# One hybrid attention block on one core: feed-forward modulation by row sums, reordered opening loads, earlier gate spills, and a root kept together at the norm

## Chip, core and metric

The kernel runs on one core of a Trainium2 chip (trn2). The metric is the device time of one execution in microseconds (us), as the median of three runs. The before kernel takes 1754.09 us (1749.22 to 1755.53). Everything is float32 with 256 tokens and a model width of 2048.

## Reference

```python
c_act = silu(c)
mod = (c_act @ ada_w + ada_b)            # 6 vectors of 2048
shift_m, scale_m, gate_m, shift_f, scale_f, gate_f = mod
h = rmsnorm(x, norm_mix_g) * (1 + scale_m) + shift_m
p = h @ w_in                             # gla q,k,v,g,gk | mla cq,ckv,kr | two gates
y_gla = (rmsnorm(gla(q,k,v,decay)) * silu(g)) @ gla_wo
y_mla = causal_mla(cq, ckv, kr) @ mla_wo
x = x + gate_m * ((sigmoid(ga)*y_gla + sigmoid(gb)*y_mla) @ w_out)
h = rmsnorm(x, norm_ffn_g) * (1 + scale_f) + shift_f
g, u = split(h @ ffn_w_in)
x = x + gate_f * ((silu(g)*u) @ ffn_w_down)
return rmsnorm(x, final_norm_g)
```

## The kernel before, in words

**Weights.** Every weight tile is loaded as 128 partitions of 1024 float32 (512 KB, `load_raw`, L102, issued by SP into a rotating list of `raw` tiles) and split in two parts: ACT casts it to a high part (L111) and DVE subtracts to a low part (L114). PE then multiplies high by high, low by high and high by low (`form_a`, L179 to L181; `form_b`, L190 to L192). One tile, called a half below, feeds 12 matmuls of 512 columns. There are three buffers for the high and the low parts.

**Stages.** (1) The opening (L429 to L474) loads x, its squares and root, transposes x with PE (`x_blocks`, L360), and works out shift and scale of the mixer. (2) The input projection runs in four rounds over the 2048 input rows, so that it can start when few rows of h exist; `jobs` is the list of 16 output blocks, `orders` the order of a round. In round 3 (the last) jobs 11 to 15 are five gate blocks, which lie in slots 4 and 6. (3) The attention: eight `mla_pair`s, with four GLA heads (`gla_att`) woven in by lanes that `tick()` advances. Pair 0 writes its projections into slot 6 (L647). (4) The GLA output gate with `gla_out` per head, then `mla_wo`, `gla_wo` and `w_out`, four blocks of eight halves each. (5) The norm, the feed-forward, and the last norm.

**Modulation.** There are two ways to a vector of `mod`. `ada_dots` (L258 to L279) loads rows of a transposed copy `ada_t`, one 512 KB tile being half of 128 rows, and makes their sums with a DVE instruction that multiplies with the broadcast `crow` and accumulates (L269): two tiles give 128 values, one per partition. It serves the mixer's shift and scale (m = 0, 1). `ada_steps` (L288 to L334) loads `ada_w` as it is, multiplies and adds on DVE (L304, two per tile), sums over partitions on POOL (`partition_all_reduce`, L314), and for m = 3 and 4 brings the result into columns with four more DVE instructions (L321). It serves m = 2 to 5. `pace` sets how many such steps a `tick()` (one per half) issues from the list `bg`; a step issues one tile.

**POOL** also does the rope angles in the opening (`rope_angles`, L364 to L400) and the root of each GLA head (`rsqrt_mean` with `G`, L213 to L216). The store of the summed gate goes out on SP (L317), the five gate spills on POOL after round 3 (L579).

**Order.** Each engine runs its instructions in one order, which a scheduler sets at build time; `keep_in_program_order` (`pin`) and `follow` bind single instructions.

Of the kernel before, what the change touches and what calls it, by code (L numbers as in the profile page):

```python
# [51 lines left out]
def tile_block(ctx: ExitStack, tc: tile.TileContext, x, positions, ada_w, ada_t, ada_b, w_in, gla_gk_w, gla_wo,  # L52
# [33 lines left out]

    def raw_tile():
# [17 lines left out]
    def split_raw(raw, kk, cols, perm=None):  # L105
# [115 lines left out]

    def rows_of(col, dst, pinned=False):
# [3 lines left out]
        for t in range(2):  # L226
            pin(V.tensor_scalar(out=d[:, t * P:(t + 1) * P], in0=ident, scalar1=col[:, t:t + 1], scalar2=None,
                                op0=ALU.mult))
# [26 lines left out]
    nc.gpsimd.dma_start(out=scr[:, 324:357], in_=cf[:, 256:289])  # L255
# [4 lines left out]
    def ada_dots(k, now=False):  # L260
        for m in (1, 0):
            c = m * 16 + k
            part = sb(1, "md", 4)
            for hf in range(2):
                raw = raw_tile()
                d = nc.sync.dma_start(out=raw, in_=ada_t[m * D + k * P:m * D + (k + 1) * P, hf * 1024:(hf + 1) * 1024])

                def dot(raw=raw, hf=hf, c=c, part=part):
                    return V.tensor_tensor_reduce(out=raw, in0=raw, in1=crow[:, hf * 1024:(hf + 1) * 1024], scale=1.0,  # L269
# [10 lines left out]

    def ada_mod(k):
        V.scalar_tensor_tensor(out=mod[:, 16 + k:17 + k], in0=mod[:, 16 + k:17 + k], scalar=1.0, in1=nmg[:, k:k + 1],
                               op0=ALU.add, op1=ALU.mult)
        modulate(k, xTk, rx, 0, hhk, hlk)

    def ada_cols(k):
        yield from ada_dots(k)
        ada_mod(k)  # L288

    def ada_steps(m, c0):  # L290
# [21 lines left out]
        if m in (2, 3, 4):  # L312
            ar = sb(512, "ada", 2)
            G.partition_all_reduce(ar, acc, channels=P, reduce_op=bass_isa.ReduceOp.add)  # L314
            yield
            if m == 2:
                tc.keep_in_program_order(nc.sync.dma_start(out=gm_sp[:, c0:c0 + cols], in_=ar[0:1]))  # L317
                return
            for i in range(nb):
                d = ar[:, i * P:(i + 1) * P]  # L320
                V.tensor_tensor_reduce(out=d, in0=d, in1=ident, scale=1.0, scalar=0.0, op0=ALU.mult, op1=ALU.add,  # L321
                                       accum_out=mod[:, b0 + i:b0 + i + 1])
            V.tensor_tensor(out=mod[:, cs], in0=mod[:, cs], in1=cb[:, cs], op=ALU.add)
# [22 lines left out]

    gm_sp = dram.tile([1, D], F32, name="gm_sp")
# [7 lines left out]
    def x_blocks(k0):  # L355
        for k in range(k0, k0 + 2, 2):
            ps = aux_bank()
            for kk in range(2):
                for t in range(2):
                    T.transpose(out=ps[:, kk * S + t * P:kk * S + (t + 1) * P],  # L360
                                in_=xtok[:, t, (k + kk) * P:(k + kk + 1) * P], identity=ident)
            A.copy(out=xT[:, k * S:(k + 2) * S], in_=ps)
# [5 lines left out]
    def rope_angles():  # L368
# [13 lines left out]
        G.dma_start(out=pos_i, in_=positions.rearrange("o (t p) -> p (o t)", p=P))  # L382
# [51 lines left out]
    more_raw((qk, 0, 4))  # L434
    first = [ada_dots(k, True) for k in range(2)]
# [9 lines left out]
    for _ in first[1]:  # L445
        pass
# [643 lines left out]
```

## Time and profile before

| | |
|---|---|
| median of three runs | 1754.09 us |
| profiled execution, its own time | 1749.99 us |
| its span | 1748.2 us |
| PE busy | 1696.2 us, 97% |
| DVE / ACT / POOL busy | 70% / 47% / 7% |
| mean granted TensorE clock | 0.986 |
| q1 (loads issued by SP) | 410.27 MB, 71.5% of 16 engines' span |

[...] The ends of matmuls are modelled, so starts are the safer reading on PE. A bracket behind a row tells how long the engine sat idle before it and what ended that; "issue" means that nothing which the profile shows was waited for.

### The profile page before, as it was taken

Reading aid. Unit: us, or ns where it says so; the run is one execution under the profiler, and the core shown is the slowest. Engines: PE = TensorE matmul, PEld = TensorE weight load, DVE = VectorE, ACT = ScalarE, POOL = GpSimd, SP = SyncE. Lnnn points to the kernel's source line nnn. Section 1 sums busy time; section 2 is a strip of 40 time slices with the busy share of each in tenths; the row PEclk is TensorE's granted clock in tenths of the full one; section 3 lists DMA queues with packets and bytes.
Section 4 is the critical chain, followed back from the end, with each engine's and each line's share of the span. In section 5 each row is a group of like instructions: output and inputs, shape, how many; then the busy total and the mean of one; then the engine's idle time right before and its main releaser. Section 6 shows DMA issues by size and latency. Waiting matters only on the chain.

```text
span 1748.2 us, 23021 instructions
## 1 busy us (share of the span) xinstructions
PE 1696.2 (97%) x8388; PEld 1428.7 (82%) x8388; DVE 1230.2 (70%) x1801; ACT 829.6 (47%) x1152; POOL 124.7 (7%) x135
## 2 busy tenths in 40 slices
PE   6999999999999999799999899999999999999997
PEld 4998899879999888588878688888888888788885
DVE  7999977587887587688999667657664444555556
ACT  5644444355767554344444554444444444444443
POOL 6200000000001021101001000000000000000000
PEclk7999999999999999899999999999999999999999
DMA  9999986665556488799999468778776666555552
GB/s 366 358 330 321 311 251 189 184 199 179 156 178 193 158 299 260 237 348 363 324 348 365 150 197 281 235 239 280 235 244 191 191 188 190 178 190 185 191 195 95
DMA packets 196074, 418.31 MB, mean 239 GB/s; under 512 B 13060, under 2 KB 23636, under 8 KB 195320
## 3 DMA queue, kind: packets, MB, share of 16 engines
q1 hardware_dynamic: 194136, 410.27, 71.5%
q0 software_dynamic: 1680, 6.51, 1.1%
q8 instruction: 66, 1.08, 0.3%
q14 instruction: 48, 0.39, 0.1%
q10 hardware_dynamic: 144, 0.07, 0.0%
HBM read 410.49 MB, written 6.30 MB: 238 GB/s over the span
## 4 chain that ended last, share of the span: by engine, by line
PE 87%; DVE 5%; DMA 3%; issue 3%; ACT 2%; POOL 0%; SPq 0%; DVEq 0%; ACTq 0%; POOLq 0%
PE mm L180 19%; PE mm L181 19%; PE mm L179 19%; PE mm L190 3%; PE mm L192 3%; PE mm L191 3%; PE mm L994 2%; PE mm L993 2%; PE mm L995 2%; DVE lo L114 2%; PE gx L711 1%; PE gx L994 1%; PE aux L994 1%; PE aux L993 1%; PE gx L993 1%
## 5 line engine op out<-in xcount | busy, mean ns | idle before, releaser
L114 DVE TENSOR_TENSOR lo<-raw,hi 128x1024 fp32r<-128x1024 f32 (+3 forms) x520 | 597.7, 1156 | 348.1 <-ACT hi L111 343.8
L111 ACT CAST hi<-raw 128x1024 fp32r<-128x1024 f32 (+3 forms) x520 | 507.8, 984 | 564.8 <-PE mm L181 417.2
L180 PE MATMUL mm<-lo,s 128*128 128x512 f32 (+1 forms) x1648 | 648.0, 393 | 9.6 <-DVE lo L114 9.5
L181 PE MATMUL mm<-hi,s 128*128 128x512 f32 (+1 forms) x1648 | 641.2, 390 | 0.0
L179 PE MATMUL mm<-hi,s 128*128 128x512 f32 (+1 forms) x1648 | 585.4, 392 | 7.5 <-ACT hi L111 5.9
L180 PEld LDWEIGHTS mm<-lo,s 128*128 128x128 f32 x1648 | 311.5, 189 | 76.5 <-DVE lo L114 14.9
L179 PEld LDWEIGHTS mm<-hi,s 128*128 128x128 f32 x1648 | 310.4, 189 | 72.2 <-ACT hi L111 7.3
L181 PEld LDWEIGHTS mm<-hi,s 128*128 128x128 f32 x1648 | 311.4, 189 | 62.6 <-issue 1.7
L304 DVE SCALAR_TENSOR_TENSOR ada<-raw,cact,ada 128x512 f32<-128x512 f32 x195 | 145.9, 748 | 15.3 <-DMA raw<-in_ada_w_dram 12.8
L190 PE MATMUL mm<-s,hi 128*128 128x256 f32 x416 | 119.1, 289 | 2.1 <-ACT s L647 2.1
L191 PE MATMUL mm<-s,hi 128*128 128x256 f32 x416 | 118.2, 286 | 0.0
L192 PE MATMUL mm<-s,lo 128*128 128x256 f32 x416 | 115.6, 286 | 0.0
L111 ACT CAST hi<-s 128x1024 fp32r<-128x1024 f32 (+1 forms) x63 | 65.1, 1036 | 94.1 <-PE mm L181 43.2
L114 DVE TENSOR_TENSOR lo<-s,hi 128x1024 fp32r<-128x1024 f32 (+1 forms) x63 | 77.5, 1230 | 31.6 <-ACT hi L111 31.4
L190 PEld LDWEIGHTS mm<-s,hi 128*128 128x128 f32 x416 | 80.1, 192 | 3.5 <-ACT s L647 2.6
L191 PEld LDWEIGHTS mm<-s,hi 128*128 128x128 f32 x416 | 80.2, 193 | 0.4
L192 PEld LDWEIGHTS mm<-s,lo 128*128 128x128 f32 x416 | 78.7, 193 | 0.3 <-DVE lo L114 0.2
L314 POOL PARTITION_ALL_REDUCE ada<-ada x12 | 46.8, 3899 | 261.2 <-DVE ada L304 251.5
L994 PE MATMUL mm<-lo,w 128*128 128x512 f32 x160 | 63.6, 398 | 0.0
L995 PE MATMUL mm<-hi,w 128*128 128x512 f32 x160 | 62.6, 393 | 0.0
L993 PE MATMUL mm<-hi,w 128*128 128x512 f32 x160 | 50.9, 396 | 0.7 <-ACT w L1002 0.7
L1002 ACT CAST w<-s 128x256 fp32r<-128x256 f32 x44 | 17.7, 407 | 61.0 <-PE aux L994 61.0
(274 smaller groups left out, 1694.8 us busy)
## 6 DMA issues: line engine op xcount, KB each, us to landing
raw<-in_ffn_w_in_dram SPq DMA_DIRECT2D x176, 512.0 KB, 4.6
raw<-in_w_in_dram SPq DMA_DIRECT2D x124, 512.0 KB, 4.9
raw<-in_ada_w_dram SPq DMA_DIRECT2D x104, 512.0 KB, 4.8
raw<-in_ffn_w_down_dram SPq DMA_DIRECT2D x88, 512.0 KB, 3.3
raw<-in_ada_t_dram SPq DMA_DIRECT2D x44, 512.0 KB, 5.6
s<-in_ada_w_dram SPq DMA_DIRECT2D x24, 512.0 KB, 6.8
s<-in_w_in_dram SPq DMA_DIRECT2D x23, 512.0 KB, 4.3
raw<-in_mla_wo_dram SPq DMA_DIRECT2D x21, 512.0 KB, 6.6
```

Source lines behind the costliest of these rows:

```text
L111: h = A.copy(out=hh_, in_=rr)
L114: V.tensor_tensor(out=ll_, in0=rr, in1=hh_.bitcast(F32), op=ALU.subtract)
L179: T.matmul(ps[t][:, :cols], lhsT=ah[:, k, ts], rhs=hi, start=st, stop=False)
L180: T.matmul(ps[t][:, :cols], lhsT=ah[:, k, ts], rhs=lo, start=False, stop=False)
L181: mm = T.matmul(ps[t][:, :cols], lhsT=al[:, k, ts], rhs=hi, start=False, stop=en)
L190: T.matmul(o, lhsT=hi[:, pick], rhs=ah[:, k], start=st, stop=False, skip_group_check=True)
L191: T.matmul(o, lhsT=hi[:, pick], rhs=al[:, k], start=False, stop=False, skip_group_check=True)
L192: T.matmul(o, lhsT=lo[:, pick], rhs=ah[:, k], start=False, stop=en, skip_group_check=True)
L304: ins = V.scalar_tensor_tensor(out=acc, in0=raw[:, k - k0], scalar=c, in1=acc, op0=ALU.mult, op1=ALU.add)
L993: T.matmul(o, lhsT=ah[:, ts], rhs=hi[:, ns], start=first, stop=False)
L994: T.matmul(o, lhsT=ah[:, ts], rhs=lo[:, ns], start=False, stop=False)
L995: T.matmul(o, lhsT=al[:, ts], rhs=hi[:, ns], start=False, stop=last)
```

## The change

The modulation of the feed-forward (m = 3, 4) moves from `ada_steps` to `ada_dots`: the host's `ada_t` now holds four of the six blocks, `crow` is stored to DRAM in the opening and read back (1 MB, broadcast to 128 partitions) ahead of `mla_wo`'s second block, and the 64 tiles are issued from there on at a pace of 0.85 instead of being queued behind m = 2 from the attention on. The roots of the GLA heads go to DVE. The gate's store goes to POOL's queue. In the opening eight tiles are given out by hand, the first two weight tiles are loaded (`pre`) ahead of the background modulation, half of x's transposes stand behind the first modulated block, and the rope angles come after round 0. Round 3 does the gate jobs right after jobs 0 to 2, and each is spilled when it is done. At the norm, copies and casts on ACT are put behind the last square and the first low parts on DVE behind the root's rows.

```diff
     def raw_tile():
+        if given:
+            return given.pop(0)
...
             h = A.copy(out=hh_, in_=rr)
+            l = V.tensor_tensor(out=ll_, in0=rr, in1=hh_.bitcast(F32), op=ALU.subtract)
             if fence:
-                follow(h, fence.pop(0))
-            V.tensor_tensor(out=ll_, in0=rr, in1=hh_.bitcast(F32), op=ALU.subtract)
+                a, b = fence.pop(0)
+                follow(h, a)
+                follow(l, b)
...
+    def ada_ffn(row):
+        for k in range(KT):
+            yield from ada_dots(k, row, (4, 3))
+            ada_scale(k, 4, nfg)
...
-        if m in (2, 3, 4):
+        if m == 2:
             ar = sb(512, "ada", 2)
             G.partition_all_reduce(ar, acc, channels=P, reduce_op=bass_isa.ReduceOp.add)
-            yield
-            if m == 2:
-                tc.keep_in_program_order(nc.sync.dma_start(out=gm_sp[:, c0:c0 + cols], in_=ar[0:1]))
-                return
-            for i in range(nb):
...
+            G.dma_start(out=gm_sp[:, c0:c0 + cols], in_=ar[0:1])
...
+        tc.keep_in_program_order(nc.sync.dma_start(out=crow_sp, in_=crow[0:1]))
...
-        for _ in range(4 - 2 * t):
+        for _ in range(4 - 3 * t):
             next(first[t])
-    for k in range(0, KT, 2):
+    for k in range(0, 8, 2):
         x_blocks(k)
...
-    ang, ang2 = rope_angles()
-    for k in range(2):
-        ada_mod(k)
+    ada_mod(0)
+    for k in range(8, KT, 2):
+        x_blocks(k, True)
+    ada_mod(1)
...
-    orders = [up[::-1], up, up[::-1], up]
+    orders = [up[::-1], up, up[::-1], up[:3] + up[11:] + up[3:11]]
...
+            if r == 3 and j >= 11:
+                (o, i), d = gates[j - 11], gdst[j - 11]
+                G.dma_start(out=spill[o][:, 1024 * i:1024 * (i + 1)], in_=d)
...
-    for b in range(4):
-        bg += [ada_steps(m, 512 * b) for m in (4, 3)]
-    pace[0] = 0.4
+    pace[0] = 0.35
...
-        rsqrt_mean(r, st, GDV, 2, G)
+        rsqrt_mean(r, st, GDV, 2)
...
-    pace[0] = 0.8
+    pace[0] = 0.85
...
+        if i == 1:
+            assert not GLA.busy()
+            row = sb(2048, "w")
+            tc.keep_in_program_order(nc.sync.dma_start(out=row, in_=crow_sp.to_broadcast([P, D])))
+            bg.append(ada_ffn(row))
...
-        A.copy(out=x1T[:, k * S:(k + 2) * S], in_=ps)
+        cp = A.copy(out=x1T[:, k * S:(k + 2) * S], in_=ps)
+        if k >= 8:
+            follow(cp, sqr)
...
-    fence[:] = [None, sqr, sqr]
+    fence[:] = [(None, None), (sqr, eye[-1]), (sqr, eye[-1])]
...
-    inputs["ada_t"] = np.asarray(inputs["ada_w"])[0, :, :2 * D].T
+    inputs["ada_t"] = np.asarray(inputs["ada_w"])[0].reshape(D, 6, D)[:, [0, 1, 3, 4]].reshape(D, 4 * D).T
```

The order of POOL's instructions around the output gate and `mla_wo`, before (L314 is the sum over partitions, L213 to L216 a head's root; a row `ISA` without tiles stands ahead of the first instruction of the other kind):

```order
L215 TENSOR_SCALAR rl<-rl 128x2
L216 TENSOR_TENSOR gr<-gr,rl 128x2
L314 ISA
L314 ISA ada<-ada 128x512
L213 ISA
L213 TENSOR_TENSOR rl<-gr 128x2
L214 TENSOR_TENSOR rl<-rl,rv 128x2
```

and with the change, from the end of the attention on (L332 is the sum, L333 the gate's store, L651 a gate's spill):

```order
L651 DMA ga_sp<-raw 128x1024
L332 ISA
L332 ISA ada<-ada 128x512
L333 DMA gm_sp<-ada 16x1x32
L720 MEMSET s_3487 128x512
L651 DMA ga_sp<-raw 128x1024
L332 ISA ada<-ada 128x512
```

The roots are gone from POOL, and so is every sum behind the fourth until the feed-forward's own.

The order of SP's loads in the opening, before (s_93 is x, L266 a modulation tile, L102 a weight tile):

```order
L437 DMA s_93<-in_x_dram 128x2048
L266 DMA raw<-in_ada_t_dram 128x1024 x2
L266 DMA s_98<-in_ada_t_dram 128x1024 x2
L102 DMA s_85<-in_w_in_dram 128x2x512
L266 DMA w<-in_ada_t_dram 128x1024
L102 DMA w<-in_w_in_dram 128x2x512
```

and with the change (L451, L275 and L106 are the same three):

```order
L451 DMA s_93<-in_x_dram 128x2048
L275 DMA s_85<-in_ada_t_dram 128x1024
L275 DMA w<-in_ada_t_dram 128x1024 x2
L275 DMA s_97<-in_ada_t_dram 128x1024
L106 DMA raw<-in_w_in_dram 128x2x512 x2
L275 DMA raw<-in_ada_t_dram 128x1024 x4
```

The first weights to be used are those in `raw`: they now stand right behind the eighth modulation tile; before, two others and four more modulation tiles were ahead of them.

The order on DVE at the norm, inside the root, before (L218 to L220 are steps of the root, L114 the low part of a weight tile; the root's rows, L227, and the first modulation, L341, follow behind two more steps):

```order
L219 SCALAR_TENSOR_TENSOR rl<-rl,rv 128x2
L114 TENSOR_TENSOR lo<-raw,hi 128x1024
L220 SCALAR_TENSOR_TENSOR rx<-rl,rx 128x2
L114 TENSOR_TENSOR lo<-raw,hi 128x1024
L218 TENSOR_TENSOR rl<-rx 128x2
L219 SCALAR_TENSOR_TENSOR rl<-rl,rv 128x2
```

and with the change, the end of the root (L224 to L226 its steps, L235 its rows, L116 the low part, L348 the first modulation):

```order
L224 TENSOR_TENSOR rl<-rx 128x2
L225 SCALAR_TENSOR_TENSOR rl<-rl,rv 128x2
L226 SCALAR_TENSOR_TENSOR rx<-rl,rx 128x2
L235 TENSOR_SCALAR e<-ident,rx 128x128 x2
L116 TENSOR_TENSOR lo<-raw,hi 128x1024 x2
L348 SCALAR_TENSOR_TENSOR e<-s_8829,mod,aux 128x256 x3
```

The two low parts of weights moved from inside the root to behind its rows, still ahead of the modulation.

## Rows read from the trace of the kernel before

**Rows 1.** The page, part 1: PE's busy time, share and instructions.
```profile
PE 1696.2 (97%) x8388; PEld 1428.7 (82%) x8388; DVE 1230.2 (70%) x1801; ACT 829.6 (47%) x1152; POOL 124.7 (7%) x135
```

**Rows 2.** Busy time by stretch of 50 us: PE, PEld, DVE, ACT, POOL, clock, DMA.
```profile
350.00:400.00 50.00, 47.17 (x260) 40.95 (x258) 42.65 (x75) 27.11 (x43) 3.19 (x6) 0.97 0.63 195
...
700.00:750.00 50.00, 40.30 (x156) 30.77 (x155) 32.69 (x55) 19.11 (x24) 6.00 (x13) 0.90 0.74 247
...
900.00:950.00 50.00, 48.95 (x223) 40.14 (x222) 47.93 (x68) 21.82 (x28) 4.20 (x1) 1.00 1.01 367
950.00:1000.00 50.00, 43.84 (x195) 35.28 (x194) 33.79 (x60) 23.11 (x36) 4.51 (x3) 0.94 0.62 218
```

**Rows 3.** The opening, timeline: start, us, engine, line, operation [idle before, releaser].
```profile
18.56 0.38 SPq L102 DMA_DIRECT2D raw<-in_w_in_dram  x1
...
22.70 1.27 DVE L269 CUSTOM_DVE_ANT_0 s<-s,s,vec 128x1024 f32<-128x1024 f32 x1
...
24.01 1.28 DVE L269 CUSTOM_DVE_ANT_0 s<-s,s,md 128x1024 f32<-128x1024 f32 x1
...
29.01 1.04 ACT L111 CAST hi<-raw 128x1024 fp32r<-128x1024 f32 x1 [2.36 <-DMA raw<-in_w_in_dram]
...
30.11 1.22 PE L179 MATMUL mm<-hi,s 128*128 128x512 f32 x2 [5.35 <-ACT hi L111]
...
30.58 1.25 DVE L114 TENSOR_TENSOR lo<-raw,hi 128x1024 fp32r<-128x1024 f32 x1
```

**Rows 4.** Busy time from the first jobs to the 368-column ones.
```profile
35.00:87.50 52.50, 52.06 (x294) 47.33 (x292) 48.56 (x73) 36.72 (x56) 17.09 (x19) 0.97 1.00 364
```

**Rows 5.** Timeline, the first attention pair's projection (ACT, then PE).
```profile
391.42 0.59 ACT L647 COPY s<-mm 128x512 f32<-128x512 f32 x1 [1.83 <-DMA ga_sp<-s]
...
392.06 0.39 PE L190 MATMUL mm<-s,hi 128*128 128x256 f32 x1 [2.14 <-ACT s L647]
```

**Rows 6.** Timeline, mla_wo's first block and after (POOL, DVE, PE).
```profile
719.91 3.25 POOL L314 PARTITION_ALL_REDUCE ada<-ada  x1 [9.72 <-issue]
730.03 0.19 POOL L216 TENSOR_TENSOR gr<-gr,rl 128x2 f32<-128x2 f32 x1 [6.87 <-issue]
...
723.19 0.29 DVE L321 CUSTOM_DVE_ANT_0 ada<-ada,ident 128x128 f32<-128x128 f32 x1 [7.06 <-POOL ada L314]
...
732.48 1.41 DVE L792 SCALAR_TENSOR_TENSOR s<-gx,gr,s 128x512 f32<-128x512 f32 x2 [6.08 <-POOL gr L216]
...
725.72 0.79 PE L180 MATMUL mm<-lo,s 128*128 128x512 f32 x1 [6.43 <-DVE lo L114]
...
733.28 0.33 PE L802 MATMUL gx<-ident,s 128*128 128x128 f32 x1 [2.21 <-DVE s L792]
```

**Rows 7.** Busy time in the stretch after the longest gap.
```profile
725.00:730.00 5.00, 4.28 (x10) 3.41 (x11) 1.40 (x3) 0.00 (x0) 0.00 (x0) 0.50 0.61 179
```

**Rows 8.** Timeline, the norm before the feed-forward (ACT, DVE, PE).
```profile
989.43 0.65 ACT L921 ACTIVATE sc<-s 128x512 f32<-128x512 f32 x1
...
991.13 1.22 DVE L114 TENSOR_TENSOR lo<-raw,hi 128x1024 fp32r<-128x1024 f32 x1
...
994.65 0.48 DVE L227 TENSOR_SCALAR e<-ident,rx 128x128 f32<-128x128 f32 x2
996.50 1.26 DVE L341 SCALAR_TENSOR_TENSOR e<-s,mod,aux 128x256 f32<-128x256 f32 x3 [1.38 <-PE aux L229]
...
997.58 0.79 PE L179 MATMUL mm<-hi,s 128*128 128x512 f32 x1 [1.11 <-ACT s L342]
```

**Rows 9.** Timeline, one old modulation step beside one weight half on DVE.
```profile
735.01 0.75 DVE L304 SCALAR_TENSOR_TENSOR ada<-s,cact,ada 128x512 f32<-128x512 f32 x1
735.67 1.22 DVE L114 TENSOR_TENSOR lo<-raw,hi 128x1024 fp32r<-128x1024 f32 x1
736.81 0.75 DVE L304 SCALAR_TENSOR_TENSOR ada<-s,cact,ada 128x512 f32<-128x512 f32 x1
```

**Rows 10.** Busy time while transposed and plain weights load together.
```profile
30.00:50.00 20.00, 19.33 (x69) 15.23 (x70) 19.24 (x27) 13.53 (x20) 18.29 (x21) 0.80 1.03 396
```

More of the change, by code (lines that the diff above doesn't have):

```diff
@@ L254, in tile_block, with ada_dots @@
     frq, sgn = scr[:, 324:356], scr[:, 356:357]
-    nc.gpsimd.dma_start(out=scr[:, 324:357], in_=cf[:, 256:289])
     mod = const.tile([P, 96], F32, name="mod")
-    def ada_dots(k, now=False):
-        for m in (1, 0):
-            c = m * 16 + k
+    T_ROW = {0: 0, 1: 1, 3: 2, 4: 3}
+    def ada_dots(k, row, ms=(1, 0), now=False):
+        for m in ms:
+            c, r0 = m * 16 + k, T_ROW[m] * D + k * P
             part = sb(1, "md", 4)
@@ L344, in modulate @@
                                op0=ALU.add, op1=ALU.subtract)
+    crow_sp = dram.tile([1, D], F32, name="crow_sp")
     gm_sp = dram.tile([1, D], F32, name="gm_sp")
@@ L353, in tile_block, with x_blocks @@
     xTk = k256(xT)
[L355 to L362, printed above, removed]
+    def x_blocks(k0, pinned=False):
+        pin = tc.keep_in_program_order if pinned else lambda i: i
+        ps = aux_bank()
+        for kk in range(2):
+            for t in range(2):
+                pin(T.transpose(out=ps[:, kk * S + t * P:kk * S + (t + 1) * P],
+                                in_=xtok[:, t, (k0 + kk) * P:(k0 + kk + 1) * P], identity=ident))
+        pin(A.copy(out=xT[:, k0 * S:(k0 + 2) * S], in_=ps))
     sin_t = const.tile([P, S], F32, name="sin_t")
@@ L433, in tile_block @@
         pin(A.copy(out=crow[:, 512 * b:512 * (b + 1)], in_=ps))
-    more_raw((qk, 0, 4))
-    first = [ada_dots(k, True) for k in range(2)]
+    wr = sb(2048, "w")
+    more_raw((scr, 3072, 1), (wr, 0, 2))
+    given += [qk[:, 1024 * i:1024 * (i + 1)] for i in range(4)]
+    given += [scr[:, 3072:4096], wr[:, 0:1024], wr[:, 1024:2048], gst[:, 0:1024]]
+    first = [ada_dots(k, crow, now=True) for k in range(2)]
     for t in range(2):
@@ L444, in tile_block @@
     rows_of(rc2, rx, pinned=True)
-    for _ in first[1]:
-        pass
-    for _ in first[0]:
-        pass
-    ang, ang2 = rope_angles()
-    for k in range(2):
-        ada_mod(k)
+    for g in first[::-1]:
+        for _ in g:
+            pass
+    ada_mod(0)
+    for k in range(8, KT, 2):
+        x_blocks(k, True)
+    ada_mod(1)
     lat = slot(4)
@@ L463, in job_half @@
         form, c0, cols, dst, scale = jobs[j]
-        (form_a if form == "a" else form_b)(ps, half(w_in, k, c0, cols), hhk, hlk, k, first, last, cols)
+        w = half(w_in, k, c0, cols) if not pre else split_raw(pre.pop(0), 2, cols)
+        (form_a if form == "a" else form_b)(ps, w, hhk, hlk, k, first, last, cols)
     up = list(range(NJ))
-    orders = [up[::-1], up, up[::-1], up]
+    orders = [up[::-1], up, up[::-1], up[:3] + up[11:] + up[3:11]]
+    spill = {O_GB: gb_sp, O_GA: ga_sp}
     hold[0] = False
@@ L471, in tile_block @@
     bg += [g for p in pairs for g in p]
-    wr = sb(2048, "w")
-    more_raw((scr, 3072, 1), (wr, 0, 2))
+    pre = [load_raw(w_in[0, 0:2 * P, jobs[j][1]:jobs[j][1] + jobs[j][2]], 2, jobs[j][2]) for j in up[:-3:-1]]
     background(2)
@@ L576, in tile_block @@
     more_raw()
-    spill = {O_GB: gb_sp, O_GA: ga_sp}
-    for (o, i), d in zip(gates, gdst):
-        G.dma_start(out=spill[o][:, 1024 * i:1024 * (i + 1)], in_=d)
     om = slot(5)
@@ L851, in tile_block @@
     gaT = slot(3)
-    pace[0] = 0.8
+    pace[0] = 0.85
     mh, ml = slot(2, F32R), slot(1, F32R)
@@ L885, in tile_block @@
     sq = sb(8, "sq")
-    pace[0] = 0.75
+    pace[0] = 0.85
     def gate_mix(i, n):
```

31 lines of the change are left out of this document (16 added, 15 removed).

## Prediction

> **What bounds the kernel now.** I read the page's first part first: PE is busy for 1696.2 of the 1748.2 us of the span [rows 1], so the number of matmuls, which the change does not touch, sets some 97% of the time. What an edit can win is only what PE waits, and what PE loses at the lower clock after a wait. The second view, busy time by stretches of 50 us, shows where that is. Most stretches have 49 to 50 us of PE; four that matter here do not: 350 to 400 us lacks 2.8 us, 700 to 750 lacks 9.7, 900 to 950 lacks 1.1 and 950 to 1000 lacks 6.2, and in three of them the mean clock is below 1.00 [rows 2]. The third view is the timeline in these places and in the opening, where the reader should look at the bracket behind a row: it tells who ended the wait. DVE is the second engine to watch: 47.9 of 50 us in the stretch at 900 us, while loads take all of the DMA time (share 1.01) [rows 2].
>
> **The change part by part.**
>
> *Opening.* PE's first projection matmul starts at 30.11 us after 5.35 us of idling, released by the cast of its weights, which had waited 2.36 us for a load that SP issued only at 18.56; the first low part follows at 30.58 [rows 3]. With the new order those weights are issued behind eight modulation tiles and are there in time. On DVE ten modulation sums stood ahead of the first low part and now eight do. Two sums are 2 x 1.31 us (from 22.70 to 24.01 [rows 3]), and some small instructions of the first modulations move behind it too, so low part and first matmul come some 4 us sooner. But the two sums are moved, not removed: round 0 still needs them, and DVE works nearly all the time from there on, 48.56 of 52.5 us [rows 4]. So the head start can be kept only as far as DVE has idle time in that stretch, 52.5 - 48.56 = 3.9 us, and the DMA share there is 1.00 already [rows 4]. I take 2.5 us of gain, between 0 (loads allow no faster pace) and 5 (the 5.35 us in front of the first matmul go and all is kept). The rope angles leave POOL's opening; four small transfers for them join SP's queue after round 0, behind the loads of tiles, and DVE needs the angles only at the start of round 3. I cost both at nothing; without that cover it would be one load's wait, some 2 us by the 2.36 of [rows 3], inside the range.
>
> *Spills.* Pair 0's copy to slot 6 waited 1.83 us for a gate's spill to land, and PE 2.14 us behind it [rows 5]. With gates done early in round 3 the five spills are old by then. The stretch has a clock of 0.97 [rows 2], that is 0.03 x 2 x 50 = 3 us at half speed, which cost half of that, 1.5. Gain 3.6 us; ends 0 (another wait in the same place, since DVE is full with the first GLA head) and 4.3 (all of the 2.8 us that the stretch lacks, and the clock).
>
> *POOL out of the way at the output gate.* Here is the largest term. A sum over partitions starts at 719.91 us after 9.72 us in which POOL waits for nothing shown; DVE, whose next instruction in order needs it, sits idle for 7.06 us, and the low part behind that leaves PE idle for 6.43. Then POOL goes back to a head's root, again after 6.87 us of nothing; DVE waits 6.08 and PE 2.21 [rows 6]. The orders above show each such change of kind on POOL preceded by an instruction without operands. In the new kernel neither the roots nor the sums of m = 3 and 4 are on POOL, so 6.43 + 2.21 = 8.6 us go. The stretch's clock is 0.90 [rows 2], 0.10 x 2 x 50 = 10 us at half speed, of which PE worked about 8: there, ten matmuls take 4.28 us, 0.43 each [rows 7], against 48.95 / 223 = 0.22 [rows 2]. So half of 8, 4 us, was lost. Gain 12.6 us, ends 8.6 (the clock falls for another reason) and 13.7 (all that PE lacks, and the clock). The roots are now 11 small DVE instructions per head in place of two; the stretches before that place have over 10 us of DVE to spare per 50, and I cost them at nothing. What is late next is a load of `mla_wo`; it has no modulation tiles ahead of it any more, since m = 2 alone is through by then.
>
> *Norm.* The last square started at 989.43 us behind two copies; two low parts, 1.22 us each, stood inside the root, whose rows began at 994.65; the first modulation started at 996.50 and PE at 997.58 [rows 8]. Without the copies the square comes about 0.9 us sooner and without the low parts the root 2.3 more. The low parts now stand between the rows and the modulation (2 x 1.14), so the modulation begins at about 994.3: a gain of 2.3 us, ends 0.9 and 4 (the clock of 0.94 [rows 2] recovers too).
>
> *The 64 feed-forward tiles.* They were spread from the attention on and now lie within 64 / 0.85 = 75 halves from `mla_wo`'s second block on. DVE pays the same per tile: 2 x 0.66 us before (735.01 to 735.67) beside 1.14 for a low part (735.67 to 736.81) [rows 9], 1.31 now [rows 3]. But there are more of them per half in this stretch: the old step list also had idle steps, so that about 0.7 tiles per half were summed there and now 0.85 are. For a `gla_wo` block DVE needs 8 x 1.14 + 6.8 x 1.31 + 4 for its results, 22.0 us, of PE's 96 x 0.22 plus transposes, about 22.5; for `w_out` it is as tight. The loads: 75 x 0.524 MB of weights, 64 x 0.524 of modulation, and 6.6 of gates, x and gains are 79.6 MB in about 206 us, 386 GB/s, where the opening moved 396 at a share of 1.03 [rows 10]. PE will wait more often than the 1.1 us of [rows 2]; I take a loss of 2.5 us, ends 0 and 9. The 1 MB for the broadcast row is in the sum; SP reaches it when the output gate leaves loads idle.
>
> [...]
>
> **The sum:** -2.5 - 3.6 - 12.6 - 2.3 + 2.5 = -18.5 us. From the profiled execution's own 1749.99 that is 1731.5. That execution lies 4.1 us below the median of the runs, so I forecast 1754.1 - 18.5 = 1735.6, rounded to **1735 us**.
>
> **The rivals.**
> *Loads or DVE bind the stage from `mla_wo` to `w_out`.* For it: share 1.01 at 367 GB/s and DVE at 96% [rows 2], with more tiles per half to come. Against it: 396 GB/s [rows 10], and longer runs of memory in the transposed copy. At 367 GB/s 79.6 MB take 217 us, 11 more than PE: 1735.6 - 2.5 + 11 = 1744. Chance 0.19 (0.05 of it for the lower rate of the rule, 1749).
> *Moved, not removed.* DVE-bound rounds swallow the opening's gain and the attention's start finds another wait (POOL's second spill stands behind loads that wait for a GLA head). Only POOL's term and the norm remain: 1754.1 - 12.6 - 2.3 + 2.5 = 1742. Chance 0.13.
> *The change does not do what it says*: the long gap stays, since DVE or a load of `mla_wo` is late in the same place. Half of its term left: 1742 too; all of it: 1748. The load of `mla_wo` would have to be 6 us late. Chance 0.05.
> *Slower.* DVE becomes the bound of the 75 halves because a sum costs more beside full loads and casts. DVE keeps up as long as 9.1 + 6.8 d + 4 is below 22.5, so up to d = 1.38 us for a sum; each 0.1 above costs 6.4 us. To lose all 21 us that the other terms give, d has to be 1.38 + 0.33 = 1.71; against it stands 1.31 [rows 3], measured while loads were full. Around 1760 at d = 1.8. Chance 0.04.
>
> **How the numbers follow.** Forecast 0.59, with a range of its own from 1726 to 1742. A measurement here can tell about 0.5% (8.8 us) from no change; 1745.3 is that bound. Forecast and the second rival lie below it, most of the first and the third too: faster 0.82, same 0.13, slower 0.05. The range reaches from the terms' better ends (-5 - 4.3 - 13.7 - 4, 1727, less 4 for the spread of the median) up to the rivals' 1747: 1723 to 1747.
>
> **What would show it.** PE's first projection matmul near 26 us; no idle piece over 1 us on PE at pair 0's projection; no POOL wait on DVE around the output gate and a stretch with 49 of 50 us of PE there; the modulation about 6 us behind the last add of x; then PE's stretches from there to the norm: below 49 they show the first rival. I am wrong if a long wait for DVE or for a load stands where POOL's was.

## Result and the profile after

| | before | after |
|---|---|---|
| median | 1754.81 us (1749.22 to 1755.61, 4 runs) | 1726.61 us (1725.4 to 1728.27, 4 runs) |
| profiled execution, its own time | 1749.99 us | 1725.5 us |
| its span | 1748.2 us | 1723.6 us |
| PE / DVE / POOL busy | 97% / 70% / 7% | 98% / 70% / 5% |

The ratio is 0.9847, with a 95% interval of 0.9823 to 0.987: the changed kernel is faster by 1.5%, 28 us by the medians. In the later comparisons the kernel before had medians of 1750.6 to 1751.2 us over 7 to 23 runs, and the changed kernel, run again, 1727.41 us: a ratio of 0.9867 (0.9853 to 0.9882). So the gain is 23 to 28 us, and the two profiled executions, 24.6 us apart in their spans, lie between. Below, what an experiment gives is its ratio times 1751 us.

The page of the kernel after, part 1 (compare [rows 1]; DVE does 24 instructions less, POOL 54 less):

```profile
PE 1686.4 (98%) x8388; PEld 1422.5 (83%) x8388; DVE 1214.2 (70%) x1777; ACT 830.1 (48%) x1152; POOL 79.1 (5%) x81
```

Busy time by stretches of 50 us, kernel after (columns as in [rows 2]):

```profile
350.00:400.00 50.00, 50.00 (x291) 44.13 (x290) 36.83 (x72) 20.77 (x38) 0.00 (x0) 1.00 0.60 185
...
700.00:750.00 50.00, 50.00 (x226) 41.46 (x225) 41.84 (x59) 24.91 (x27) 0.00 (x0) 1.00 1.00 376
...
850.00:900.00 50.00, 48.28 (x221) 39.10 (x220) 45.57 (x65) 21.03 (x26) 0.00 (x0) 1.00 0.99 365
900.00:950.00 50.00, 49.53 (x220) 40.46 (x219) 39.56 (x52) 22.52 (x28) 0.00 (x0) 1.00 0.96 337
950.00:1000.00 50.00, 44.88 (x198) 36.21 (x197) 34.99 (x66) 28.09 (x43) 1.09 (x2) 0.93 0.47 154
```

The stretches 350 to 400 and 700 to 750 us, which lacked 2.8 and 9.7 us of PE, have all of it now, at a clock of 1.00. Of the four that lacked PE before, only the norm's is left with a low clock, 0.93, and the crowded loads from 700 us on, at 361 to 376 GB/s up to 900 us, cost PE little.

Where the time went is best read from the same piece of work in both traces. Kernel before, timeline: the last matmul of the input projection's 368-column job, the last attention projection, the last block of the output gate, the first of `mla_wo`, the last but one of `w_out` (the norm's first matmul is in [rows 8]):

```profile
264.06 0.33 PE L181 MATMUL gx<-hi,s 128*128 128x368 f32 x1
...
590.58 0.28 PE L664 MATMUL mm<-hi,s 128*128 128x256 f32 x1
...
698.52 1.26 ACT L820 COPY s<-mm 128x512 f32<-128x512 f32 x2
...
740.72 1.28 DVE L849 TENSOR_TENSOR s<-mm,s 128x512 f32<-128x512 f32 x2
...
985.80 0.69 DVE L919 TENSOR_TENSOR sc<-mm,s 128x512 f32<-128x512 f32 x1 [2.00 <-PE mm L181]
```

And the same five in the timeline of the kernel after:

```profile
259.38 0.33 PE L187 MATMUL gx<-hi,s 128*128 128x368 f32 x1
...
582.26 0.28 PE L679 MATMUL mm<-hi,s 128*128 128x256 f32 x1
...
690.78 1.27 ACT L833 COPY s<-mm 128x512 f32<-128x512 f32 x2 [0.94 <-PE mm L187]
...
718.93 1.28 DVE L867 TENSOR_TENSOR s<-mm,s 128x512 f32<-128x512 f32 x2
...
963.20 0.69 DVE L937 TENSOR_TENSOR sc<-mm,s 128x512 f32<-128x512 f32 x1 [2.00 <-PE mm L187]
```

The leads are 4.7, 8.3, 7.7, 21.8 and 22.6 us; at the first feed-forward matmul the lead is 24.1 us, at the end 24.6. So 4.7 us came from the opening, 3.6 between there and the attention's last projection, 0.6 was given back at the attention's end, 14.1 came at `mla_wo`'s first block, 0.8 over the stage with the 64 tiles, 1.5 at the norm, and 0.5 after it.

The opening of the kernel after, timeline (compare [rows 3]):

```profile
9.74 1.67 SPq L106 DMA_DIRECT2D raw<-in_w_in_dram  x2
...
21.58 1.05 ACT L115 CAST hi<-raw 128x1024 fp32r<-128x1024 f32 x1
...
23.41 1.22 PE L185 MATMUL mm<-hi,s 128*128 128x512 f32 x2 [0.42 <-ACT s L349]
...
24.34 1.22 DVE L116 TENSOR_TENSOR lo<-raw,hi 128x1024 fp32r<-128x1024 f32 x1
...
34.01 0.50 PE L186 MATMUL mm<-lo,s 128*128 128x512 f32 x1 [1.65 <-DVE lo L116]
```

The first weights are issued at 9.74 us, were issued at 18.56, and PE starts 6.7 us sooner. When the second round begins 4.3 of these are left, and 4.7 at the end of the input projection. The wait of 1.65 us at 34.01 is the longest there; the eight transposes that moved behind the first modulated block also stand on PE there now, 1.60 us from 24.42 on. Against both stands the clock, in the ten microseconds from the first weight matmul, before and after (columns as in [rows 2]):

```profile
30.11:40.11 10.00, 9.44 (x26) 7.02 (x27) 10.00 (x13) 5.21 (x8) 9.26 (x10) 0.61 1.04 398
...
23.41:33.41 10.00, 8.92 (x34) 6.41 (x34) 10.00 (x18) 6.91 (x13) 0.00 (x0) 0.89 1.03 401
```

In both traces the granted clock is 1.00 or 0.50 and nothing between: at 0.50 it stands from 27.64 to 37.88 us before and from 15.33 to 25.57 after. That is 7.8 us at half speed before and 2.2 after in these ten microseconds, so some 2.8 us less lost, by an estimate from these two rows.

The attention's end in the kernel after, timeline of ACT and PE, the one place that got worse:

```profile
592.10 0.60 ACT L801 ACTIVATE sc<-gx 128x512 f32<-128x512 f32 x1
...
592.68 0.80 ACT L628 ACTIVATE sc<-sc,st 128x128 f32<-128x128 f32 x2
...
593.13 0.33 PE L633 MATMUL aux<-ident,sc 128*128 128x128 f32 x1 [2.15 <-ACT sc L628]
```

The last head's scores are scaled on ACT (L628) behind copies of another job and a square of the output gate (L801), and PE waits 2.15 us. Before, PE's longest wait here was 0.60 us.

The norm in the kernel after, timeline (compare [rows 8]):

```profile
966.35 0.64 ACT L939 ACTIVATE sc<-s 128x512 f32<-128x512 f32 x1
...
967.43 2.01 ACT L115 CAST hi<-raw 128x1024 fp32r<-128x1024 f32 x2
...
969.71 0.48 DVE L235 TENSOR_SCALAR e<-ident,rx 128x128 f32<-128x128 f32 x2 [0.27 <-DVE rx L226]
969.98 0.42 PEld L954 LDWEIGHTS aux<-ident,s 128*128 128x128 f32 x4 [1.96 <-ACT s L958]
969.98 0.66 PE L954 MATMUL aux<-ident,s 128*128 128x128 f32 x4 [1.72 <-ACT s L958]
970.11 2.35 DVE L116 TENSOR_TENSOR lo<-raw,hi 128x1024 fp32r<-128x1024 f32 x2
...
972.38 1.25 DVE L348 SCALAR_TENSOR_TENSOR e<-s,mod,aux 128x256 f32<-128x256 f32 x3
...
973.45 0.80 PE L185 MATMUL mm<-hi,s 128*128 128x512 f32 x1 [2.28 <-ACT s L349]
```

From the last square to the rows of the root it takes 3.4 us now and took 5.2, but from the rows to the first modulation 2.7 where it took 1.9: two low parts stand there.

### The profile page after: what moved, and what is told of

Read it like the earlier page. It is cut to its first block, busy times and chain, and to the rows that moved or that the text cites. A ratio compares the mean times of both kernels' runs of the same rounds, so it can differ in the third digit from the quotient of the medians.

```text
span 1723.6 us, 22892 instructions
## 1 busy us (share of the span) xinstructions
PE 1686.4 (98%) x8388; PEld 1422.5 (83%) x8388; DVE 1214.2 (70%) x1777; ACT 830.1 (48%) x1152; POOL 79.1 (5%) x81
## 3 DMA queue, kind: packets, MB, share of 16 engines
q0 software_dynamic: 1744, 6.50, 1.0%
## 4 chain that ended last, share of the span: by engine, by line
PE 94%; DVE 3%; DMA 1%; ACT 1%; issue 1%; SPq 0%; DVEq 0%; ACTq 0%
PE mm L186 21%; PE mm L187 21%; PE mm L185 21%; PE mm L197 3%; PE mm L198 3%; PE mm L196 3%; PE mm L1013 2%; PE mm L1015 2%; PE mm L1014 2%; PE gx L726 2%; PE gx L1014 1%; PE aux L1014 1%; PE gx L1013 1%; PE aux L1015 1%; PE gx L1015 1%; PE aux L1013 1%
## 5 line engine op out<-in xcount | busy, mean ns | idle before, releaser
L116 DVE TENSOR_TENSOR lo<-raw,hi 128x1024 fp32r<-128x1024 f32 (+3 forms) x518 | 590.2, 1146 | 358.6 <-ACT hi L115 355.5
L322 DVE SCALAR_TENSOR_TENSOR ada<-raw,cact,ada 128x512 f32<-128x512 f32 x120 | 89.7, 748 | 13.4 <-DMA raw<-in_ada_w_dram 11.6
L116 DVE TENSOR_TENSOR lo<-s,hi 128x1024 fp32r<-128x1024 f32 (+1 forms) x65 | 78.1, 1203 | 24.2 <-ACT hi L115 23.7
L514 DVE TENSOR_TENSOR s<-mm,s 128x512 f32<-128x512 f32 (+1 forms) x62 | 40.0, 673 | 0.7 <-PE mm L187 0.4
```

Source lines behind the costliest of these rows:

```text
L116: l = V.tensor_tensor(out=ll_, in0=rr, in1=hh_.bitcast(F32), op=ALU.subtract)
L322: ins = V.scalar_tensor_tensor(out=acc, in0=raw[:, k - k0], scalar=c, in1=acc, op0=ALU.mult, op1=ALU.add)
```

## The experiments

### Roots on DVE, alone

The kernel before with one edit:

```diff
-        rsqrt_mean(r, st, GDV, 2, G)
+        rsqrt_mean(r, st, GDV, 2)
```

> The kernel before with one edit: the roots of the GLA heads on DVE, as in the change; the sums of m = 2, 3 and 4 stay on POOL. Theory A (what costs is POOL changing between roots and sums): POOL now has only sums there, the 9.72 us and 6.87 us of nothing ahead of them go, and with them PE's waits of 6.43 and 2.21 us and the low clock: 12 to 16 us less than before, about 1740. Rival B (what costs is DVE standing in order behind a sum at all, whatever POOL did before it): DVE still has to wait for ten sums, PE still waits 3 to 6 us at mla_wo, and the gain is 0 to 5 us, 1750 or more. Rival C (the load of mla_wo is late there as well): as B, but PE waits for a cast that waits for a load.

Measured: 1735.24 us, ratio 0.9916 (0.9902 to 0.993), 14.7 us less. POOL in this kernel, timeline:

```profile
659.43 4.12 POOL L314 PARTITION_ALL_REDUCE ada<-ada  x1 [36.48 <-DVE ada L304]
707.91 3.23 POOL L314 PARTITION_ALL_REDUCE ada<-ada  x1 [44.35 <-DVE ada L304]
```

This is theory A. All sums are still there, m = 3 and 4 among them, but they wait for their input alone. The idle pieces of [rows 6] that nothing explained are gone, and with them PE's 6.43 and 2.21 us. This single edit gives over half of what the whole change gives.

### Row sums, alone

The kernel before with m = 3 and 4 by `ada_dots` from `mla_wo`'s second block on; the roots stay on POOL, the gate's store on SP.

```diff
-        if m in (2, 3, 4):
+        if m == 2:
...
+            bg.append(ada_ffn(row))
...
-    for b in range(4):
-        bg += [ada_steps(m, 512 * b) for m in (4, 3)]
-    pace[0] = 0.4
+    pace[0] = 0.35
```

> The kernel before with the feed-forward's shift and scale by ada_dots from mla_wo's second block on (paces as in the change), the roots still on POOL and the gate's store still on SP. Theory A: the last two changes of kind on POOL come with m = 2's sums during the output gate, before the place of the long gap; PE's wait for a sum at 720 us is gone, but a head's root can still be late by a change (7 to 10 us, of which some is covered): 8 to 15 us less than before. Rival B: all of it, 13 to 16 us less, since no DVE instruction stands behind a sum any more. If the dense tiles bind (rival D), the gain is 2.5 to 9 us smaller than either says.

Measured: 1737.71 us, ratio 0.9928 (0.9915 to 0.994), 12.6 us less. One bad place is left, earlier than before (timeline of POOL, DVE and PE):

```profile
673.58 3.25 POOL L325 PARTITION_ALL_REDUCE ada<-ada  x1 [23.46 <-DVE ada L315]
686.08 0.18 POOL L213 TENSOR_TENSOR rl<-gr 128x2 f32<-128x2 f32 x1 [9.25 <-issue]
...
689.34 1.41 DVE L794 SCALAR_TENSOR_TENSOR s<-gx,gr,s 128x512 f32<-128x512 f32 x2 [7.47 <-POOL gr L216]
...
690.15 0.33 PE L804 MATMUL gx<-ident,s 128*128 128x128 f32 x1 [3.14 <-DVE s L794]
```

A root that came just behind a sum was held up by 9.25 us for which the profile has no cause, DVE by 7.47 and PE by 3.14. That is theory A's root that is late by a change. So row sums win by taking sums out of the roots' way, as roots on DVE do: 12.6 and 14.7 are largely the same microseconds, as the last experiment shows.

### Opening, spills and norm, each alone

The kernel before with the new opening (loads given out by hand, half of the transposes later, rope angles after round 0):

```diff
+    given += [qk[:, 1024 * i:1024 * (i + 1)] for i in range(4)]
+    given += [scr[:, 3072:4096], wr[:, 0:1024], wr[:, 1024:2048], gst[:, 0:1024]]
...
-    ang, ang2 = rope_angles()
-    for k in range(2):
-        ada_mod(k)
+    ada_mod(0)
+    for k in range(8, KT, 2):
+        x_blocks(k, True)
+    ada_mod(1)
...
+    pre = [load_raw(w_in[0, 0:2 * P, jobs[j][1]:jobs[j][1] + jobs[j][2]], 2, jobs[j][2]) for j in up[:-3:-1]]
...
+            ang, ang2 = rope_angles()
```

> The kernel before with the opening alone: tiles by hand, the two first weight tiles ahead of the background, half of the transposes behind the first modulated block, rope angles after round 0. Theory A: the terms add, and this one gives what the changed kernel's trace shows at the start of round 1, 4.3 us: 1748 to 1751 against 1754.8, first projection matmul at 23.4 us. Rival B: DVE or the loads take the head start back by round 3 when the rest is unchanged: 0 to 1.5 us less.

Measured: 1746.09 us, ratio 0.9974 (0.9966 to 0.9983), 4.6 us less (3.0 to 6.0), as theory A has it (4.3), with the first projection matmul at 23.23 us.

The kernel before with the gates early in round 3:

```diff
-    orders = [up[::-1], up, up[::-1], up]
+    orders = [up[::-1], up, up[::-1], up[:3] + up[11:] + up[3:11]]
...
+            if r == 3 and j >= 11:
+                (o, i), d = gates[j - 11], gdst[j - 11]
+                G.dma_start(out=spill[o][:, 1024 * i:1024 * (i + 1)], in_=d)
```

> The kernel before with round 3 in the new order and each gate spilled when done. Theory A: the 2.14 us wait at pair 0 goes with the low clock behind it (1.5 us): 2 to 4 us less than before. Rival B: the attention's start finds other waits, since DVE is full with the first GLA head: 0 to 1 us. Rival C (GLA's preparation moves into round 3, where DVE has room, which helps beyond pair 0): 5 to 6 us.

Measured: 1745.93 us, ratio 0.9978 (0.9969 to 0.9987), 3.9 us less (2.3 to 5.4). The waits of [rows 5] are gone, the stretch from 350 to 400 us has 50.00 us of PE at a clock of 1.00, and no wait takes their place. That is theory A's 2 to 4 us; the interval leaves some room for rival C's 5.

The kernel before with the norm's edits:

```diff
-    fence[:] = [None, sqr, sqr]
+    fence[:] = [(None, None), (sqr, eye[-1]), (sqr, eye[-1])]
...
+        if k >= 8:
+            follow(cp, sqr)
```

> The kernel before with the change's edits at the feed-forward norm alone: the two rows of ones behind the root held together, the order of squares, copies and weight splits at the norm as in the changed kernel. My theory (the prediction's norm term): the first feed-forward matmul comes 2 us earlier, 1 to 3 us less in all (0.05 to 0.2%). Rival, from comparing the two traces, where the stretch from the last eviction of w_out to the first feed-forward matmul is only about 1.5 us shorter: 0.5 to 1.5 us, not to be told from no change; PE still waits 1.7 us for a copy behind two casts and some 2 us for the modulation.

Measured: 1750.2 us beside 1751.17, ratio 0.9994 (0.9985 to 1.0003): 1.1 us, not to be told from none. The rival, drawn from the two traces, had the size right.

### The changed kernel again, and its roots back on POOL

> The changed kernel, unaltered, as the baseline for the three kernels beside it on the same chip. Expected 1725 to 1728 us, a ratio to the kernel before of 0.984 to 0.987. No theory differs here.

Measured: 1727.41 us, ratio 0.9867 (0.9853 to 0.9882), as expected.

```diff
-        rsqrt_mean(r, st, GDV, 2)
+        rsqrt_mean(r, st, GDV, 2, G)
```

> The changed kernel with one thing undone: the roots of the output gate go back to POOL, while the four column sums of the attention gate stay there and the feed-forward modulation stays off it. Theory A (POOL loses 7 to 10 us each time it goes from column sums to roots or back while a root is waited for): there are now fewer changes of kind than before, because only 4 sums are left; each one that falls ahead of a root shows as POOL idle of 7 to 10 us that nothing in the profile explains, a DVE wait of some 7 us for the root, and a PE wait of 2 to 6 us if it comes late in the stage. Time 2 to 8 us above the changed kernel. Rival: what cost time was the 12 sums themselves and their number alone; then with 4 sums the roots on POOL cost nothing (0 +- 1 us).

Measured: 1727.51 us, ratio 0.9867 (0.9852 to 0.9882): no loss. My figure of 2 to 8 us was wrong. POOL in this kernel, timeline (L332 is a sum, L219 the start of a root):

```profile
617.57 4.11 POOL L332 PARTITION_ALL_REDUCE ada<-ada  x1 [10.49 <-DVE ada L322]
...
642.04 0.19 POOL L219 TENSOR_TENSOR rl<-gr 128x2 f32<-128x2 f32 x1 [19.36 <-DVE gr L215]
```

Sums and roots still alternate, but the root comes 20 us after the sum and starts at once when DVE has its input. So a change of kind by itself did not cost anything; either it is done during that wait, or the sums' number is what counts. The next pair tells these apart.

### A sum directly ahead of each root, and directly behind it

Both: the changed kernel with roots on POOL, and one small sum more per block of the gate.

```diff
+        x = sb(8, "st", 2)[:, 0:2]
+        G.partition_all_reduce(x, st, channels=P, reduce_op=bass_isa.ReduceOp.add)
         rsqrt_mean(r, st, GDV, 2, G)
```

> The changed kernel with the roots of the output gate on POOL, as in the run before where that cost nothing, and one more column sum on POOL per block of the gate (of the block's two sums of squares; its result is not used), placed directly ahead of the block's root: it can start only when the root's input is nearly ready. Theory A (after a sum POOL needs 7 to 10 us, whatever it waits for meanwhile, until an elementwise instruction runs; a root that comes later than that loses nothing): each of the four roots starts 9 to 13 us late (the sum's own 1 to 4 us and 7 to 10 us shown as idle with nothing that the profile explains), DVE waits on POOL for it, PE stands 2 to 7 us in each of the four blocks: 12 to 30 us above the changed kernel. Rival B (what cost time is the number of sums or POOL's own work): the root is late by the sum's 1 to 4 us only, and the time within 3 us of the changed kernel, the same as for the run with the sums behind the roots.

```diff
         rsqrt_mean(r, st, GDV, 2, G)
+        x = sb(8, "st", 2)[:, 0:2]
+        G.partition_all_reduce(x, r, channels=P, reduce_op=bass_isa.ReduceOp.add)
```

> The same four more column sums on POOL and the same roots there, but each sum placed directly behind its block's root, some 25 us ahead of the next one (it sums the root itself; its result is not used). As many sums and changes of kind as in the run beside it; only the distance from a sum to the next root differs. Theory A: the 7 to 10 us after each sum lie in the time in which POOL waits for the next block, so nothing is lost: within 1.5 us of the changed kernel, no PE wait above 1 us between 600 and 740 us. Rival B: as long as the run beside it.

Measured: ahead 1744.89 us, ratio 0.9954 (0.994 to 0.9968); behind 1728.5 us, ratio 0.9869 (0.9856 to 0.9883). As many sums, 16 us apart. With the sums ahead, the last block (timeline of POOL, DVE, PE; L803 is the added sum):

```profile
705.26 2.46 POOL L803 PARTITION_ALL_REDUCE st<-gst  x1 [16.23 <-ACT sc L801]
719.62 0.19 POOL L219 TENSOR_TENSOR rl<-gr 128x2 f32<-128x2 f32 x1 [11.90 <-issue]
...
722.90 1.41 DVE L807 SCALAR_TENSOR_TENSOR s<-gx,gr,s 128x512 f32<-128x512 f32 x2 [11.14 <-POOL gr L222]
...
723.71 0.47 PE L817 MATMUL gx<-ident,s 128*128 128x128 f32 x1 [6.82 <-DVE s L807]
```

The same rows exist for all four blocks: from the sum's end to the root 7.58, 8.81, 7.78 and 11.90 us of idle time without a cause. PE stood still for 0.58 + 0.33, 3.16 and 6.82 us in the second to the fourth block and not at all in the first, less than the 2 to 7 us in each that I expected; these waits, 10.9 us, and the half clock behind them (a mean of 0.97 from 650 to 700 us and of 0.93 from 700 to 750, so, by an estimate from these two, 10 us at half speed, or 5 lost) make the 16 us. With the sums behind (L804):

```profile
685.68 1.31 POOL L804 PARTITION_ALL_REDUCE st<-gr  x1 [6.36 <-issue]
699.80 0.20 POOL L219 TENSOR_TENSOR rl<-gr 128x2 f32<-128x2 f32 x1 [12.81 <-DVE gr L215]
```

Here POOL idles for 6.36 us between root and sum, which delays nobody, and the next root starts as soon as its input is there. So the number of sums is not the cost. The added sums' own time also delays the roots that stand behind them, by 0.84, 0.41, 0.84 and 2.46 us; the larger part of each delay, 6 to 12 us in all these kernels, comes with the change of kind. It is free when it falls into a wait of POOL and delays the root when that stands right behind a sum. Nor is it the sum itself that runs on unseen: in [rows 6] DVE starts on the sum's result at 723.19 us, 0.03 us behind the sum's shown end, and the root still waits until 730.03.

What stands at the start of these microseconds the traces hold, although the rows of the views leave it out: at each change of kind two instructions MODIFY_POOL_CONFIG of 0.1 us or less, in the place of the unnamed `ISA` rows of POOL's order. In the kernel before they start at 723.11 and 723.15 us, where the sum ends at 723.16. They come when the last instruction of the old kind ends, not when the first of the new kind has its input: at 707.71 us with the sums ahead, where the sum ends at 707.72, and at 624.41 in the kernel before, where the sum ends at 624.43 and POOL's wait for the root's input only at 647.26. That is why a wait of POOL hides the change. From the second of the two to the next sum or elementwise instruction it took from 5.94 to 11.92 us where POOL did not wait longer for something else (6.89 from 723.15 to 730.03 in the kernel before). There are 20 of them in the kernel before and in this pair, 16 with the roots back on POOL, and 4 in the changed kernel and in the one with roots on DVE alone.

What fills the microseconds behind them stays open. The page shows no transfers that go with them: the two queues for instructions carried 66 and 48 packets in the kernel before, which has 20 such instructions, and 66 and 47 in the changed kernel, which has 4.

### More modulation tiles per half

The changed kernel with the pace raised in the three stages from `mla_wo` to `w_out`:

```diff
-    pace[0] = 0.85
+    pace[0] = 1.2
```

> The changed kernel with the pace of the modulation's 64 tiles raised from 0.85 to 1.2 per step in the three stages from mla_wo to w_out: the same loads and dot-sums, crowded into some 70% of the stretch. It asks how near the loads or DVE are to setting the time there. By the rows of the changed kernel (361 to 376 GB/s at a busy share of 1.00, DVE 42 to 46 us of 50) the demand in the crowded part is worked out as some 430 GB/s. Theory L (the loads are at their limit at 376 to 396 GB/s, and the 64 tiles just fit): some 8 to 20 us slower, PE waiting on the casts or low parts of late weights in that part. Rival N (the queues are only kept full ahead of need, and there is room): within 2 us of the changed kernel, with a shown rate above 400 GB/s. Rival D (DVE binds first): slower, with DVE at 49 us or more of 50 and PE waiting on low parts whose tiles were loaded long before.

Measured: 1734.82 us, 7.4 more than the changed kernel beside it; ratio to the kernel before 0.9912 (0.9897 to 0.9926). Busy time by stretch:

```profile
750.00:800.00 50.00, 49.05 (x212) 39.11 (x211) 47.34 (x67) 20.45 (x20) 0.00 (x0) 1.00 1.04 399
800.00:850.00 50.00, 46.10 (x194) 36.71 (x193) 47.88 (x71) 19.53 (x22) 0.00 (x0) 0.93 1.04 398
```

The loads do not pass 399 GB/s, where by the estimate 430 were asked for, and DVE reaches 47.9 of 50 us: both are near their end, PE loses 3.9 us in the second stretch, and rival N is out. PE's four longest waits in these stages, 0.79 to 2.04 us, were all ended by DVE, three by a low part and one by a result; but ACT's casts waited for their loads up to 5.4 us, so which of the two ends first this run does not settle. It shows how near the changed kernel is to that end: at 0.85 the rows show up to 376 GB/s without a loss on PE, and at 1.2 they show 399 with one.

### Splits behind the modulation at the norm

The changed kernel with casts and low parts moved once more:

```diff
-    fence[:] = [(None, None), (sqr, eye[-1]), (sqr, eye[-1])]
+    fence[:] = [(None, None), (cp, ml[0]), (cp, ml[2])]
```

> The changed kernel, with the first two weight splits of the feed-forward product behind the last copy of the transposed x on ACT (the casts) and behind modulations 0 and 2 on DVE (the low parts); no arithmetic changes. Theory: at the norm PE waits 1.72 us for a copy that stands behind two casts (2.01 us on ACT) and then 2.28 us for the first modulation, which stands behind two low parts (2.35 us on DVE). With both out of the way the first feed-forward matmul comes 2 us earlier, and with it the end: 1.5 to 3 us less than the changed kernel beside it (0.1 to 0.2%). Rival: the splits are then late, and PE waits for the first low part instead, at the first L186 behind the norm: no gain (0 +- 1 us).

Measured: 1726.78 us, 0.6 under the changed kernel beside it, which no measurement here can tell from nothing. PE in this kernel, timeline:

```profile
972.50 0.94 PE L237 MATMUL aux<-e,ones 128*128 128x256 f32 x2 [1.62 <-ACT hi L115]
974.56 0.79 PE L185 MATMUL mm<-hi,s 128*128 128x512 f32 x1 [1.11 <-ACT s L349]
```

The waits of 1.72 and 2.28 us became 1.62 and 1.11: the wait for a copy is gone, and one at the root's rows (L237) is there in its place. From PE's wait at the attention's end to this matmul it takes 379.3 us, and 380.4 in the changed kernel run again: 1.1 us are won, not 2.

### All parts but the row sums

The kernel before with opening, spills, roots on DVE and the norm as in the change, and the modulation as it was.

```diff
-            yield from ada_dots(k, row, (4, 3))
...
+    for b in range(4):
+        bg += [ada_steps(m, 512 * b) for m in (4, 3)]
+    pace[0] = 0.4
```

(against the changed kernel)

> The changed kernel without its first part: opening, early spills, roots on DVE and the norm as in the change, but the feed-forward's shift and scale by the old steps, with their sums on POOL, queued behind the gate's from the attention on (and the gate's store on SP, as before). It asks what the move to row sums is worth once the roots are off POOL. My theory from the runs before: it is worth nothing, or costs 1 to 3 us. The four other parts alone gave, by their ratios, 4.6 + 3.9 + 14.7 + 1.1 = 24.3 us; the changed kernel gave 23.3 in the same way. So 1726 us, 1724 to 1728, a ratio of 0.985 to 0.987, without the 2.15 us wait at the attention's end, which appears wherever the row sums are in. Rival: the sums on POOL and their four instructions on DVE still cost something between 600 and 980 us, or the parts' gains overlap: 1731 to 1735 us.

Measured: 1727.08 us, ratio 0.9859 (0.9839 to 0.9879). That is 24.7 us less than the kernel before (21.2 to 28.2), where the changed kernel again gave 23.3 (20.7 to 25.7) and the four parts one by one 24.3: the parts add up, and the part that stands first in the change shows no gain of its own once the roots are off POOL. In PE's timeline at the attention's end the wait is short:

```profile
595.67 0.72 PE L185 MATMUL mm<-hi,s 128*128 128x512 f32 x2 [0.60 <-ACT hi L115]
```

## Why the prediction was right, and where it was off

The direction, the place and the mechanism were right, and 1726.6 us lies inside the range, 8.4 us below the forecast of 1735 and just above the lower end, 1726, of the forecast's own range. Most terms came out better than forecast, and only the norm's worse. By term, in us:

| term | forecast (ends) | alone on the chip | between the two traces |
|---|---|---|---|
| opening | -2.5 (0 to -5) | -4.6 | -4.7 |
| spills | -3.6 (0 to -4.3) | -3.9 | -3.6 |
| POOL out of the way | -12.6 (-8.6 to -13.7) | -14.7 (roots only) | -14.1 |
| norm | -2.3 (-0.9 to -4) | -1.1 | -1.5 |
| 64 tiles | +2.5 (0 to 9) | about 0 (all parts with and without row sums) | +0.6 at the attention's end, -0.8 in their stage |
| after the norm | none | | -0.5 |
| sum | -18.5 | -24.3 for the first four | -24.6 |

- **POOL's term** was right in kind: a change of kind on POOL, then DVE, then PE. I took 8.6 us for the two waits and 4 for half speed; 13.7, the end, counts in all of the 9.7 us that PE lacks in the stretch. The two traces (14.1) and the single edit (14.7, 12.3 to 17.2) stand just past that end, while 12.6 lies inside the edit's interval: if it was too small, the two long waits alone were too little, for 1.1 us are shorter waits in the same stretch. What the prediction did not see is that either of two parts does it alone: roots on DVE, or row sums with one wait left. It counted them as one term, so the sum was not hurt. "Late next" was a load of `mla_wo`; none came late, and the stretch has 50.00 us of PE.
- **Spills** were right: the wait at pair 0 is gone. The new wait at the attention's end, 2.15 us, is not the "another wait" of the second rival: it appears in every kernel with row sums, also in the one with row sums alone and the spills as before (2.16), and in none without them (0.60).
- **The opening** was mis-sized, by the step that said the head start can be kept only as far as DVE idles behind it, with loads at share 1.00 allowing little. The first matmul came at 23.41, not "near 26", and 4.7 of the 6.7 us were kept. The term also had nothing for the clock, which gave back some 2.8 us in the first ten microseconds (0.61 to 0.89, above; 0.86 with the opening alone). Busy time in the kernel after from the first matmul to the end of round 0:

```profile
23.40:83.20 59.80, 56.84 (x311) 49.37 (x311) 57.54 (x89) 40.82 (x63) 6.34 (x7) 0.98 1.02 383
```

  DVE idles 2.3 us of 59.8, and the loads move 383 GB/s at a share of 1.02, where [rows 4] had 364 at 1.00. A share of 1.00 was not the limit that I took it for; [rows 10] had shown 396 already.
- **The 64 tiles** were mis-sized the other way, by the step that set a row sum of 1.31 us beside a low part of 1.14 and left POOL out of it. A row sum took 1.28 us, and a low part in the stage from `mla_wo` to `w_out` became cheaper, 1.22 us where it was 1.29 and 1.27: POOL's sums no longer run beside it (below). The tiles fit, at 361 to 376 GB/s, with waits on PE of 1.05, 0.68 and 0.47 us. What the row sums did cost is the wait at the attention's end, which no term had.
- **The norm** was half to two thirds of what I said, by the two steps that put the square 0.9 us sooner and the root another 2.3: by the traces, from the last but one result of `w_out` (985.80, now 963.20) to the last square 0.5 us are won, 3.15 where it was 3.63, and from there to the root's rows 1.9. The two low parts between rows and modulation cost 0.8 of it, much as counted (0.9). That leaves 1.5. PE's new wait of 1.72 us for a copy behind two casts is not on this path: the modulation starts at 972.38 without idling behind the low parts.
- **The start.** I set the sum against the median of 1754.1. The kernel before has a median near 1751 in three longer series, so some 3 us of the miss are the start's, and 6 the terms' (9 together, as the forecast was 1735.6 before it was rounded). The range's upper end, 1747, is called the rivals', but none of them stands there: they gave 1742, 1744, 1748 and 1749, and 1760.
- **The rivals.** Loads or DVE as the bound, 0.19, did not come at this pace, but begin between 0.85 and 1.2 tiles per half: the run at 1.2 lost 7.4 us, where I had priced 11 for 0.85. No run shows the lower rate of loads that stands behind the 0.05 and the 1749: the stage moved 361 to 376 GB/s up to 900 us, and 398 to 399 at a pace of 1.2. "Moved, not removed", the long gap that stays, and DVE slower than 1.38 us per sum were all refuted by the rows above.

## What to carry to other kernels

When one engine idles for several microseconds for no cause that the profile shows, look at what kind of instruction stood before the gap and after it; if the kind changes (on POOL here 6 to 12 us each time), either move one kind to another engine or put the change where the engine would wait anyway. Price such an edit from the waits of the engine at the end of the chain, the short ones beside the long ones too, plus the low clock behind them (0.50 from 725 to 730 us in [rows 7]). And try the cheapest part of a change alone: here one argument of one call gave 14.7 of some 24 us, and the largest part of the code nothing that could be told on top of it.

## What the runs showed of the hardware

**A sum over partitions on POOL can hold DVE up.** In the kernel without row sums, timeline of POOL and DVE:

```profile
831.32 3.53 POOL L321 PARTITION_ALL_REDUCE ada<-ada  x1 [27.74 <-DVE ada L311]
...
831.67 3.26 DVE L116 TENSOR_TENSOR lo<-raw,hi 128x1024 fp32r<-128x1024 f32 x1
```

The low part ends 0.08 us behind the sum. The same low part takes 1.22 us elsewhere; others beside a sum in this kernel took 1.68, 1.93, 2.67 and 2.73. Not each one is held up: in the kernel before, eight of the 24 low parts of 128x1024 beside a sum took 1.69 to 3.26 us and the other 16 1.21 to 1.23, while away from the sums none took more than 1.33. In the changed kernel, which has no sums in this stage, the longest there takes 1.23.

**The same wait does not always cost the clock.** PE's wait of 2.15 to 2.16 us at the attention's end was followed by a granted clock of 1.00 in the changed kernel in two profiled executions, and of 0.89 over the 15 us around it in the kernels with row sums alone, with sums ahead of and behind the roots, and with the pace of 1.2. By an estimate from that 0.89, some 3.3 us ran at half speed and 1.6 were lost, or not, and no run here shows why.
